# A sixth pair of gates by seven products, weights split ahead, and the attention bias by transfer, in a transformer layer

## The chip, the cores and the metric

The kernel runs on one core of a Trainium2 chip. The metric is the device time of one execution in microseconds (us), as the median of several runs. One further execution is recorded by the hardware profiler; all rows of the profile come from that one. Engines: PE is TensorE (matrix multiplication; PEld is its weight load), DVE is VectorE, ACT is ScalarE, POOL is GpSimd, and SP is the engine that issues all transfers here. "SPq" rows are its queue.

## The reference

One layer over 1024 tokens of width 1024. Two kinds of attention run side by side on the same input, and two sigmoid gates merge them:

```python
h = x @ w_in[l]
qa, ka, va, qb, kb, vb, ga, gb = jnp.split(h, split_pts, axis=-1)
y_a = chunk_band_attention(heads_a(qa), heads_a(ka), heads_a(va), rel_bias[l]) @ w_proj_a[l]
y_b = stick_breaking_attention(heads_b(qb), heads_b(kb), heads_b(vb)) @ w_proj_b[l]
gate_a = jax.nn.sigmoid(ga + b_gate[l, :D])
gate_b = jax.nn.sigmoid(gb + b_gate[l, D:])
mix = (gate_a * y_a + gate_b * y_b) @ w_out[l]
x = layer_norm(DEEPNORM_ALPHA * x + mix, ln1_g[l], ln1_b[l])
gu = x @ w_ffn_in[l]
g, u = jnp.split(gu, 2, axis=-1)
ffn = (jax.nn.silu(g) * u) @ w_ffn_out[l]
x = layer_norm(DEEPNORM_ALPHA * x + ffn, ln2_g[l], ln2_b[l])
```

Attention A (8 heads of 64) is a softmax over a band of 9 chunks of 64 tokens, with a learned bias `rel_bias[head, clip(distance)]` added to each score. Attention B (8 heads of 64) is strictly causal and has no softmax: a weight is a sigmoid times the running product of (1 - sigmoid) over the keys between. All values are float32.

## The kernel before

**Matmuls.** A float32 operand is split into a high and a low part (`split`, line 108: a ScalarE copy that rounds, and a VectorE subtraction for the rest). Each product is three matmuls: high x high, high x low, low x high. The whole program is laid out by a scheduler when it is built: it orders the instructions of each engine from the order in the code, the data they need and the buffers that come free. So the order in the code is a priority, and an instruction that is ready can move ahead of one that is not.

**Buffers.** On-chip memory is divided into tags (`SLOTS`, line 42) of equal buffers of 128 x 1024. Tags `qs`, `kh`, `kl` and `v` have two each; the helper `cycle` (line 71) deals them in turn during the projections, and attention uses the same tags for the heads' q, k (high), k (low) and v. PSUM has 8 banks (`BANKS`, line 43): 2 for fillers and products, 2 for scores, 3 for transposes, 1 for the value sum (`pv`).

**Projections.** The list `work` (line 228) has a pair of column panels per entry: q with k of two heads, v with v, and gate A with gate B. Each pair is computed by a seven-product scheme (`pair_steps`, line 183; products in the order 1, 2, 6, 5, 7, 3, 4) in place of eight: 7 x 12 = 84 matmuls of 512 columns in place of 96. Product 6 adds into the PSUM bank that ScalarE copied out after product 1. `run_pairs` (line 410) runs the list and loads the next weights in between. `N_GATE = 5` (line 236) gate pairs, ten of sixteen gates, are done here, and their sigmoid too (`out_g`, line 394). `small_inputs` (line 315) brings in the bias table, reversed, and the gate biases. Results go to memory and are loaded again per head.

**Attention.** `vsteps` (line 800) is a hand-written list of 12 steps a head: 8 in the first half of the queries (g = 0) and 4 in the second (g = 1). In each step the loop at line 821 does, in this order: due loads; due score blocks (`LEAD`, line 37, tells how many blocks must be out by which of the 12 steps); the step's transposes (`turn`, line 648) with their split on ScalarE and VectorE; some fillers; the value matmul (`mult`, line 657) of the step `LAG` = 2 back; some more fillers. The first `mult` of a half needs the one `pv` bank, which ScalarE empties after the last `mult` of the half before (line 679).

In A a score block (`soft_block`, line 573) is a sum with the bias and a running minimum on VectorE (line 582), an exponential on ScalarE (line 588), a reciprocal, and a division on GpSimd (line 593). The bias of a head (`rel_bias_tile`, line 556) is loaded with one row per partition, shifted by one, and then turned round and negated by ScalarE (line 562). In B a block (`stick_block`, line 607) is two sigmoids on ScalarE, a scan on VectorE and a product on GpSimd (line 628).

**Fillers.** `fill_all` (line 695) yields single matmuls of work that depends on no attention step: the gates that the projections left out (`gate`, line 453, 48 matmuls each) and then the projection of A's output (line 732, 24 for each of eight panels). `FILL = (18.0, 42.0)` is how many of them go to a head of A and of B. Their weights are loaded, copied by ScalarE (line 439) and subtracted by GpSimd (line 440) while attention runs. `later` (line 630) holds work that is due some steps on: the addition of the two halves of a head's output (line 683) and then, for the last pairs of heads, the split of that output (`split_y`, line 765: a ScalarE copy and a GpSimd subtraction).

After attention come the projection of B's output, the output projection, the first normalization, and the feed-forward part, which the change does not touch.

Of the kernel before, what the change touches and what calls it, by code (L numbers as in the profile page):

```python
# [11 lines left out]
F32 = mybir.dt.float32  # L12
F32R = mybir.dt.float32r
# [20 lines left out]


LAG = 2
LEAD = ((6, 7, 9, 9, 10, 10, 11, 11, 12, 12, 13, 13), (7, 8, 9, 9, 10, 10, 11, 11, 12, 12, 13, 14))

FILL = (18.0, 42.0)

# [5 lines left out]
def hybrid_trunk_kernel(ctx: ExitStack, tc, x, xt, w_in, b_gate, rel_bias, w_proj,  # L48
# [55 lines left out]
    ORDER = (1, 2, 6, 5, 7, 3, 4)  # L104
    s_dr = [[dram(f"s_dr{g}_{hf}_", 7) for hf in range(2)] for g in range(4)]
    rel_dr = dr.tile([8, 896], F32, name="rel_dr")

    def split(dst_h, dst_l, src):
        nc.scalar.copy(dst_h, src)  # L109
# [123 lines left out]
            if i % 2:  # L233
                work.append(("v", br * 4 + i - 1, br * 12 + 8 + i - 1, br * 12 + 8 + i))

    N_GATE = 5
    work += [("g", j, 24 + j, 32 + j) for j in range(N_GATE)]
    Wa = [dict() for _ in work]

# [3 lines left out]
    def right(i):  # L243
        prep_right(Wa[i], f"p{i}", w_in[work[i][3]], "op")
        prep_last(Wa[i], f"p{i}", "kp")
# [69 lines left out]
    def small_inputs():  # L315

        rel_sb = cycle(QKV, "rel_sb")[0:8, 0:896]
        rel_in = cycle(QKV, "rel_in")[0:8, 0:N_REL]
        dma(rel_in, rel_bias)
        nc.vector.tensor_copy(rel_sb[:, 383:896], rel_in[:, ::-1])  # L320
        nc.vector.tensor_copy(rel_sb[:, 0:383], rel_in[:, 512:513].to_broadcast([8, 383]))
        dma(rel_dr, rel_sb)
        dma(bg, b_gate)

    def store_hl(d, hi, lo):
# [30 lines left out]
    def project(i):  # L356
# [50 lines left out]

        return pair_steps(f"p{i}", Wa[i], ops_x, c, done, "pv" if i == 3 else "mm")

    def run_pairs(steps, left, right, also=lambda i: None, first=2, aside=lambda i: None,  # L410
                  then=lambda: None):

        n = len(steps)
        for j in range(first):
            steps[j][0]()
            steps[j][1]()
        then()
        for i in range(n):
            rest = steps[i][2:] if i < first else steps[i]
            for j, p in enumerate(rest):  # L420
                p()
                if j == 0 and i + 1 < n:
                    right(i + 1)
                if j == 1 and i + 2 < n:
                    left(i + 2)
                aside(i)
            also(i)
# [16 lines left out]
    def load_w(*args):  # L444
        return begin_w(*args)()

    def of(tag):
        return lambda name, dtype=F32: slot(tag, name, dtype)

    def begin_gate(i, lo_eng):  # L450
        return begin_w(w_in[24 + (i % 2) * 8 + i // 2], f"g{i}", of("op"), of("op"), lo_eng)

    def gate(i, w, half_way, freed=None):
# [49 lines left out]
    def rest_of_start():  # L503
# [3 lines left out]
        for kt in range(4):  # L507
# [2 lines left out]

    run_pairs([project(i) for i in range(1, len(work))],
              lambda i: left(i + 1) if i > 2 else left_again(3) if i == 2 else None,
              lambda i: right(i + 1), first=3, then=rest_of_start, also=lambda i: small_inputs() if i == 2 else None)
    first_gate = 2 * N_GATE
    first_w = begin_gate(first_gate, nc.vector)()


# [36 lines left out]
        return [t[0][:, 0:512], t[0][:, 512:896], t[1][:, 0:256], t[1][:, 256:384]]  # L554

    def rel_bias_tile(head):
        braw = slot("kp", f"braw{head}")
        src = rel_dr[head:head + 1, 0:640]
        dma(braw[:, 0:640],
            bass.AP(tensor=src.tensor, offset=src.offset, ap=[[1, P], [1, 640]]))  # L560
        bias = slot("kp", f"bias{head}")
        nc.scalar.activation(bias[:, 0:640], braw[:, 0:640][:, ::-1], AF.Copy, scale=-1.0)  # L562
        nc.gpsimd.memset(bias[0:DH, 576:640], BIG)  # L563
        nc.gpsimd.memset(bias[DH:P, 0:DH], BIG)
        return bias
# [66 lines left out]
    def value_steps(hd, g, wt):  # L632

        br, h = hd["br"], hd["h"]
        reach = (4, 8)[br]
        q0 = 4 * g
        nm = f"{'ab'[br]}{hd['n']}_{g}"
        pv = []

        kbs = [4, 5, 6, 7, 3, 2, 1, 0] if g == 0 else [7, 6, 5, 4]  # L640
        steps = []
        for i, kb in enumerate(kbs):
            lo_q = max(q0, kb - reach)
            hi_q = min(q0 + 3, kb)
            n = (hi_q - lo_q + 1) * P
            pts = []

            def turn(kb=kb, lo_q=lo_q, hi_q=hi_q, n=n, pts=pts):
                tp = bank("tr", f"tp_{nm}_{kb}")
                for qb in range(lo_q, hi_q + 1):  # L650
                    tr(tp[:, (qb - lo_q) * P:(qb - lo_q + 1) * P],  # L651
                       wt[qb - q0][:, (kb - qb) * P:(kb - qb + 1) * P], ident)
                pt = slot("pt", f"pt_{nm}_{kb}", F32R)
                split(pt[:, 0:n], pt[:, HW:HW + n], tp[:, 0:n])
                pts.append(pt)

            def mult(i=i, kb=kb, lo_q=lo_q, n=n, pts=pts):
                v = hd["v"]
                if i == 0:
                    pv.append(bank("pv", f"pv_{nm}"))  # L660
                last = i == len(kbs) - 1
                cs = slice((lo_q - q0) * P, (lo_q - q0) * P + n)
                pt = pts[0]
                mm(pv[0][:, cs], v[:, kb, :], pt[:, 0:n], start=(i == 0), stop=False)
                mm(pv[0][:, cs], v[:, kb, :], pt[:, HW:HW + n], start=False, stop=last)
                if last:
                    yt = hd["yt"]()
                    r = slice(h * DH, (h + 1) * DH)
                    gs = slice(g * HW, (g + 1) * HW)
                    if hd["i"] == 7:  # L670
                        nc.scalar.copy(yt[r, gs], pv[0][DH:P])
                        nc.vector.tensor_tensor(yt[r, gs], pv[0][0:DH], yt[r, gs], ALU.add)
                    else:

                        if g == 0:
                            hd["yv"] = slot("yt", f"yv_{nm}")
                        yv = hd["yv"]
                        both, other = (yt, yv) if h == 0 else (yv, yt)
                        nc.scalar.copy(both[:, gs], pv[0])
                        dma(other[r, gs], both[(DH, 0)[h]:(P, DH)[h], gs])  # L680

                        def add():
                            nc.gpsimd.tensor_tensor(yt[r, gs], yt[r, gs], yv[r, gs], ALU.add)
                            if h == 1 and g == 1:
                                if hd["i"] > 4:
                                    later.append([2, lambda: split_y(hd["i"], yt, nc.gpsimd)])
                                else:
                                    dma(y_dr[hd["i"]], yt)
                        later.append([3, add])

            steps.append((turn, mult))
        return steps


    def fill_all():
        w = first_w
        got = []
        for i in range(first_gate, 15):
            end = begin_gate(i + 1, nc.gpsimd)
            yield from gate(i, w, lambda: got.append(end()))  # L700
            w = got.pop()
        end = begin_proj(0, 0, "op", nc.gpsimd)
        ends = {}

        def freed(k):
# [9 lines left out]
        gates = {0: begin_gA(0)}  # L715
        for cc in range(4):
            if cc < 3:
                end = begin_proj(0, cc + 1, "op", nc.gpsimd)
            for j in range(2):
                c = 2 * cc + j  # L720
                t = gates.pop(c)
# [99 lines left out]
    for si, (hd, g, st, box) in enumerate(vsteps):  # L821
# [18 lines left out]
        goal += FILL[hd["br"]] / nhead  # L840
        fill_until(0.5 * (last + goal))
        pend.append(mult)
        if len(pend) > LAG:
            pend.pop(0)()
        fill_until(goal)
    for m_ in pend:
# [391 lines left out]
```

## Time and profile before

| What | us |
|---|---|
| median of 3 runs | 1454.58 (1454.35 to 1455.19) |
| the profiled execution | 1453.11 |
| its span, first to last instruction | 1451.1 |

The span falls into stages; TensorE's busy time in those that the change does not touch:

| Stage | from, to | TensorE busy |
|---|---|---|
| start | 0 to 30.0 | 28.07 of 30.0 |
| rest of B's output, output projection, first normalization | 662 to 812 | 149.00 of 150.0 |
| feed-forward, first part | 812 to 1207 | 395.00 of 395.0 |
| feed-forward, second part, and the end | 1207 to 1451.1 | 234.71 of 244.1 |

How to read rows: in a row by stretches, "393.89:409.90 16.01, 15.56 (x96) ..." is the stretch, its length, and then busy time (and number of instructions) of each engine named in the text. A row of waits has who waited, for whom, the total, how often, and the longest. A busy TensorE overlaps one matmul with the next, so spacing, not duration, is what a matmul costs.

### The profile page before, as it was taken

To read this page: it belongs to the slowest core of one execution; us is meant where nothing else is said; L and a number is where in the kernel's file an instruction comes from. 1 tells how busy PE (TensorE), PEld (TensorE's weight loads), DVE (VectorE), ACT (ScalarE), POOL (GpSimd) and SP (SyncE) were. 2 spreads that over 40 slices of the span, in tenths; PEclk is the share of its full clock that TensorE was granted. 3 is DMA by queue.
4 is the path that set the end of the run, shared out by engine and by line. 5 is a ranking of instruction groups with operands and counts; after the bars stand their busy time and mean duration, and the time that the engine had idled before them with its cause. 6 is when DMAs were issued, how large, how long until landed. Compare 5 with 4: busy or idle time off the path is not lost.

```text
span 1451.1 us, 19140 instructions
## 1 busy us (share of the span) xinstructions
PE 1429.5 (99%) x6748; PEld 1181.2 (81%) x6748; DVE 1024.4 (71%) x1644; ACT 682.7 (47%) x1187; POOL 278.9 (19%) x326
## 2 busy tenths in 40 slices
PE   9999999999999999999999999999999999999997
PEld 7888888888888788877888888888888887888886
DVE  8875565434776878877849966676677755978767
ACT  6444444446878878874313633444444433221201
POOL 0000000003655879850014000000000000100016
PEclk9999999999999999999999999999999999999999
DMA  7555545338667477647502123344444457787602
GB/s 247 156 178 174 174 148 186 110 101 255 196 191 199 131 226 229 204 178 239 186 25 94 66 102 114 134 159 160 160 159 145 151 197 250 286 307 242 205 15 102
DMA packets 83167, 246.15 MB, mean 170 GB/s; under 512 B 10480, under 2 KB 10480, under 8 KB 83072
## 3 DMA queue, kind: packets, MB, share of 16 engines
q1 hardware_dynamic: 83072, 244.94, 50.8%
q8 instruction: 53, 0.87, 0.2%
q14 instruction: 42, 0.34, 0.1%
HBM read 161.51 MB, written 79.72 MB: 166 GB/s over the span
## 4 chain that ended last, share of the span: by engine, by line
PE 90%; DVE 4%; ACT 2%; issue 1%; DMA 1%; POOL 1%; SPq 0%; POOLq 0%; DVEq 0%; ACTq 0%
PE sxf L179 15%; PE sxp L179 12%; PE szf L179 7%; PE dx L1171 6%; PE szp L179 6%; PE syf L179 4%; PE gps L460 4%; PE syp L179 3%; PE dz L1171 3%; PE yAps L732 2%; PE tp_b L651 2%; PE ops L119 2%; PE ops L117 2%; PE ops L116 2%; PE fpswh_h L116 2%; PE fpswh_h L119 2%
## 5 line engine op out<-in xcount | busy, mean ns | idle before, releaser
L1127 POOL TENSOR_TENSOR wdyt<-wdyt 128x512 f32<-128x512 f32 x8 | 10.7, 1336 | 515.7 <-DVE wdgt L1126 485.1
L628 POOL TENSOR_TENSOR w_b<-w_b,kp_b 128x511 f32<-128x511 f32 (+3 forms) x96 | 97.4, 1029 | 26.9 <-DVE kp_b L623 16.9
L623 DVE TENSOR_TENSOR_SCAN kp_b<-kp_b,ident_ps 128x512 f32<-128x512 f32 (+2 forms) x64 | 56.5, 883 | 24.9 <-ACT kp_b L620 24.6
L891 POOL TENSOR_TENSOR mv<-mv,neghalf 128x1 f32<-128x1 f32 x16 | 23.9, 1491 | 210.9 <-DVE mv L890 210.9
L563 POOL MEMSET bias<- 64x64 f32 x8 | 1.2, 145 | 327.8 <-ACT bias L562 327.8
L192 DVE TENSOR_TENSOR c<-sxp,c 128x512 f32<-128x512 f32 x16 | 11.1, 691 | 69.8 <-issue 40.2
L620 ACT ACTIVATE kp_b<-sc_b 128x512 f32<-128x512 f32 (+3 forms) x96 | 48.4, 504 | 23.9 <-PE sc_b L546 22.9
L110 DVE TENSOR_TENSOR pt_b<-tp_b,pt_b 128x512 fp32r<-128x512 f32 (+1 forms) x96 | 50.3, 543 | 8.4 <-ACT pt_b L109 7.7
L179 PE MATMUL szf<-x1S63h,wcf 128*128 128x512 f32 x168 | 55.1, 389 | 0.0
L1102 DVE TENSOR_TENSOR x<-dx,x 128x512 f32<-128x512 f32 x64 | 43.2, 686 | 15.5 <-PE dx L1171 15.5
L110 DVE TENSOR_TENSOR sl<-h,sl 128x512 fp32r<-128x512 f32 x56 | 38.4, 685 | 19.4 <-ACT sl L109 19.4
L593 POOL TENSOR_SCALAR w_a<-w_a,st_a 128x640 f32<-128x640 f32 (+2 forms) x64 | 42.8, 671 | 48.2 <-DVE st_a L592 33.0
L110 DVE TENSOR_TENSOR pt_a<-tp_a,pt_a 128x512 fp32r<-128x512 f32 (+1 forms) x96 | 45.8, 486 | 8.1 <-ACT pt_a L109 6.9
L651 PE MATMUL tp_b<-ident,w_b 128*128 128x128 f32 x288 | 47.7, 274 | 3.7 <-DVE pt_b L110 3.4
L109 ACT CAST pt_b<-tp_b 128x512 fp32r<-128x512 f32 (+1 forms) x96 | 47.3, 499 | 8.2 <-PE tp_b L651 7.4
L109 ACT CAST sl<-h 128x512 fp32r<-128x512 f32 x56 | 34.7, 620 | 33.7 <-PE syf L179 17.1
L116 PE MATMUL ops<-wh_o,mh 128*128 128x512 f32 x128 | 50.2, 392 | 0.0
L119 PE MATMUL ops<-wh_o,ml 128*128 128x512 f32 x128 | 50.0, 391 | 0.0
L117 PE MATMUL ops<-wl_o,mh 128*128 128x512 f32 x128 | 49.9, 390 | 0.0
L621 ACT ACTIVATE w_b<-sc_b 128x511 f32<-128x511 f32 (+3 forms) x96 | 48.5, 506 | 0.0
L109 ACT CAST pt_a<-tp_a 128x512 fp32r<-128x512 f32 (+1 forms) x96 | 40.0, 426 | 18.2 <-PE tp_a L651 16.9
L588 ACT ACTIVATE w_a<-w_a,st_a 128x640 f32<-128x640 f32 (+2 forms) x64 | 44.7, 698 | 5.2 <-DVE st_a L582 4.3
(1890 smaller groups left out, 4807.2 us busy)
## 6 DMA issues: line engine op xcount, KB each, us to landing
s_dr<-sl SPq DMA_DIRECT2D x112, 256.0 KB, 2.3
sd<-s_dr SPq DMA_DIRECT2D x56, 512.0 KB, 4.5
wLf<-in_w_ffn_in_dram SPq DMA_DIRECT2D x22, 512.0 KB, 4.5
wRf<-in_w_ffn_in_dram SPq DMA_DIRECT2D x22, 512.0 KB, 3.6
wRp<-in_w_in_dram SPq DMA_DIRECT2D x17, 512.0 KB, 4.7
wLp<-in_w_in_dram SPq DMA_DIRECT2D x17, 512.0 KB, 5.4
v_dr<-v SPq DMA_DIRECT2D x16, 512.0 KB, 4.5
kl<-k_dr SPq DMA_DIRECT2D x32, 256.0 KB, 5.4
```

What stands on the lines that cost most here:

```text
L109: nc.scalar.copy(dst_h, src)
L110: nc.vector.tensor_tensor(dst_l, src, dst_h.bitcast(F32), ALU.subtract)
L116: mm(acc, lh, rh, start=(i == 0), stop=False)
L117: mm(acc, lh, rl, start=False, stop=False)
L119: mm(acc, ll, rh, start=False, stop=(i == n))
L179: mm(acc, lw[:, ks], rx, start=(first and kt == i == 0), stop=(kt == 3 and i == 2), skip_group_check=not first)
L460: mm(acc[hf], lw[:, ks], rx[k][:, (LO, HI)[hf]], start=(k == j == 0), stop=(k == KT - 1 and j == 2))
L621: nc.scalar.activation(be[:, m0:e], sc[:, m0 - c0:n], AF.Sigmoid)
L623: nc.vector.tensor_tensor_scan(kp[:, 0:e], kp[:, 0:e], ident_ps()[:, 0:e], 0.0, ALU.mult, ALU.add)
L628: nc.gpsimd.tensor_tensor(be[:, m0:e], be[:, m0:e], kp[:, m0 - 1:e - 1], ALU.mult)
L651: tr(tp[:, (qb - lo_q) * P:(qb - lo_q + 1) * P], wt[qb - q0][:, (kb - qb) * P:(kb - qb + 1) * P], ident)
L1171: mm(acc, a, b, start=(first and i == n == 0), stop=(i == n - 1 == 1), skip_group_check=not first)
```

## The change

- `N_GATE` goes from 5 to 6: gates 10 and 11 move from the fillers to the seven-product list.
- `FILL` goes from (18, 42) to (8, 40): 8 x (8 + 40) = 384 fillers, 96 fewer.
- The weights of the fillers but the first gate's (gates 13, 14, 15 and four pairs of panels for A's output) are loaded, split and stored to memory in the last seven steps of the projections (`store_split`), and loaded in two parts when they are needed (`begin_split`).
- The bias table is negated by ScalarE when it is brought in, and not reversed. Eight transfers from memory to memory write it 128 times per head, each row one place further (a step of 1025 in rows of 1024). `rel_bias_tile` is then one plain load, without ScalarE's turn.
- `LEAD`: one score block of A a step earlier. In A the first value matmul of a head's second half is held back by one step, and two follow in the next. The split of an output of B waits 6 steps after its addition, not 2.

```diff
-LEAD = ((6, 7, 9, 9, 10, 10, 11, 11, 12, 12, 13, 13), (7, 8, 9, 9, 10, 10, 11, 11, 12, 12, 13, 14))
-FILL = (18.0, 42.0)
+LEAD = ((6, 8, 9, 9, 10, 10, 11, 11, 12, 12, 13, 13), (7, 8, 9, 9, 10, 10, 11, 11, 12, 12, 13, 14))
+FILL = (8.0, 40.0)
...
+    skew_dr = [dr.tile([P + 1, 1024], F32, name=f"skew_dr{h}") for h in range(8)]
...
-    N_GATE = 5
+    N_GATE = 6
...
-        nc.vector.tensor_copy(rel_sb[:, 383:896], rel_in[:, ::-1])
-        nc.vector.tensor_copy(rel_sb[:, 0:383], rel_in[:, 512:513].to_broadcast([8, 383]))
+        nc.scalar.activation(rel_sb[:, 0:513], rel_in, AF.Copy, scale=-1.0)
+        nc.scalar.activation(rel_sb[:, 513:896], rel_in[:, 512:513].to_broadcast([8, 383]),
+                             AF.Copy, scale=-1.0)
         dma(rel_dr, rel_sb)
+        for h in range(8):
+            src, dst = rel_dr[h:h + 1, 128:896], skew_dr[h][0:1, 128:896]
+            dma(bass.AP(tensor=dst.tensor, offset=dst.offset, ap=[[1025, P], [1, 768]]),
+                bass.AP(tensor=src.tensor, offset=src.offset, ap=[[0, P], [1, 768]]))
...
+    first_gate = 2 * N_GATE
+
+    def aside_work(i):
+        if i == 2:
+            small_inputs()
+        first = len(work) - 1 - len(ws_dr)
+        if i >= first:
+            store_split(i - first)
...
+    ws_dr = [dram(f"ws_dr{i}_", 2) for i in range(15 - 2 * N_GATE + 4)]
+
+    def store_split(i):
+        n = 15 - 2 * N_GATE
+        if i < n:
+            j = 2 * N_GATE + 1 + i
+            srcs = w_in[24 + (j % 2) * 8 + j // 2]
+        else:
+            srcs = [(cs, w_proj[2 * (i - n) + j][:, 0:HW]) for j, cs in enumerate((LO, HI))]
+        take = lambda name, dtype=F32: cycle(QKV, name, dtype)
+        for d, t in zip(ws_dr[i], load_w(srcs, f"pre{i}", take, take, nc.vector)):
+            dma(d, t.bitcast(F32))
+
+    def begin_split(i, name):
+        hl = [slot("op", f"w{p}_{name}", F32R) for p in "hl"]
+        for d, t in zip(ws_dr[i], hl):
+            dma(t.bitcast(F32), d)
+        return lambda: hl
...
     def begin_gate(i, lo_eng):
+        if i > first_gate:
+            return begin_split(i - first_gate - 1, f"g{i}")
...
-              lambda i: right(i + 1), first=3, then=rest_of_start, also=lambda i: small_inputs() if i == 2 else None)
-    first_gate = 2 * N_GATE
+              lambda i: right(i + 1), first=3, then=rest_of_start, also=aside_work)
...
-        braw = slot("kp", f"braw{head}")
-        src = rel_dr[head:head + 1, 0:640]
-        dma(braw[:, 0:640],
-            bass.AP(tensor=src.tensor, offset=src.offset, ap=[[1, P], [1, 640]]))
         bias = slot("kp", f"bias{head}")
-        nc.scalar.activation(bias[:, 0:640], braw[:, 0:640][:, ::-1], AF.Copy, scale=-1.0)
+        dma(bias[:, 0:640], skew_dr[head][0:P, 256:896])
...
-                                    later.append([2, lambda: split_y(hd["i"], yt, nc.gpsimd)])
+                                    later.append([6, lambda: split_y(hd["i"], yt, nc.gpsimd)])
...
-        end = begin_proj(0, 0, "op", nc.gpsimd)
+        end = begin_split(15 - first_gate, "y0_0")
...
-                end = begin_proj(0, cc + 1, "op", nc.gpsimd)
+                end = begin_split(16 - first_gate + cc, f"y0_{cc + 1}")
...
-        if len(pend) > LAG:
+        wait = hd["br"] == 0 and (g, st) == (1, LAG)
+        while len(pend) > LAG + wait:
             pend.pop(0)()
```

## The prediction

> **What bounds the kernel now.** I read the page's first part, then the chain of work that ended last, then the busy time by stage.
>
> ```profile
> span 1451.1 us, 19140 instructions
> PE 1429.5 (99%) x6748; PEld 1181.2 (81%) x6748; DVE 1024.4 (71%) x1644; ACT 682.7 (47%) x1187; POOL 278.9 (19%) x326
> PE 90%; DVE 4%; ACT 2%; issue 1%; DMA 1%; POOL 1%; SPq 0%; POOLq 0%; DVEq 0%; ACTq 0%
> ...
> 30.00:342.90 312.90, 312.77 (x1409) 257.89 (x1408) 180.63 (x243) 141.52 (x198) 2.99 (x5) 1.00 0.52 160
> 342.90:483.00 140.10, 135.35 (x816) 114.79 (x815) 107.12 (x366) 116.23 (x286) 82.10 (x115) 1.00 0.67 195
> 483.00:662.00 179.00, 174.58 (x969) 146.43 (x969) 141.32 (x204) 139.58 (x307) 132.15 (x165) 1.00 0.61 191
> ```
>
> TensorE carries 90% of the chain. The three stretches are the projections, attention A and attention B; their columns are length, then busy time of TensorE, weight load, VectorE, ScalarE and GpSimd, then clock, DMA share and GB/s. Outside the projections the other engines are close behind: in A VectorE and ScalarE are busy for 107 and 116 of 140 us. So a matmul taken out is worth its spacing only while TensorE stays the last engine, and I read the stages one by one.
>
> Two rows of the chain in order of time give the spacing in the projections:
>
> ```profile
> 332.30 2.72 PE szp L179 x12
> 335.02 2.72 PE sxp L179 x12
> ```
>
> Twelve matmuls of 512 columns take 2.72 us, or 0.2267 us each. For A I cut the stage into heads, from one first value matmul of a second half to the next; the second group of rows counts only the gate fillers of line 460. The last row is one B head.
>
> ```profile
> 363.39:377.51 14.12, 13.47 (x87) 11.81 (x87) 11.77 (x47) 12.23 (x34) 9.16 (x14) 1.00 0.69 190
> 393.89:409.90 16.01, 15.56 (x96) 13.57 (x96) 12.27 (x46) 13.00 (x33) 7.98 (x13) 1.00 0.84 250
> 409.90:425.91 16.01, 15.55 (x96) 13.56 (x96) 12.27 (x46) 12.58 (x33) 8.24 (x13) 1.00 0.62 183
> ...
> 342.90:363.39 20.49, 8.20 (x25) 4.32 (x25) 1.00 0.81 238
> ...
> 363.39:377.51 14.12, 3.99 (x9) 1.70 (x9) 1.00 0.69 190
> 393.89:409.90 16.01, 7.60 (x18) 3.40 (x18) 1.00 0.84 250
> ...
> 528.00:550.00 22.00, 22.00 (x125) 18.62 (x124) 16.83 (x24) 20.05 (x44) 19.64 (x24) 1.00 0.79 249
> ```
>
> These rows already hold the main experiment. A head with 18 fillers takes 16.01 us; one that happened to get 9 took 14.12. Nine fillers are worth 1.89 us, against 9 x 0.2267 = 2.04 by spacing. VectorE is busy for 12.27 us of a head: that is the floor if TensorE gets out of its way.
>
> **The change part by part.**
>
> *Gate pair six.* Two gates leave the attention fillers: 2 x 48 = 96 matmuls, 80 of them from A (8 heads x 10) and 16 from B (8 x 2). They come back as seven products of 12, 84 matmuls, in the projections, where TensorE has no gaps: +84 x 0.2267 = +19.04 us. Out of A go 80 x 0.2267 = 18.14, out of B 16 x 0.2267 = 3.63. Net -2.72 us if every filler was on the path. With 8 fillers an A head would take 14.12 - 0.23 = 13.89 us, still 1.6 above VectorE's floor.
>
> *Shifted steps in A.* The change issues one score block a step earlier and holds the first value matmul of a head's second half back by one step. The waits of A:
>
> ```profile
> PEld sc_a L545 <- DVE st_a L582: 4.7, 11, 0.7
> PEld pv_a L664 <- ACT yt L679: 2.5, 5, 0.8
> PE sc_a L545 <- DVE st_a L582: 2.0, 6, 0.5
> PEld pv_a L664 <- ACT yv_a L679: 1.4, 3, 0.5
> PE pv_a L664 <- ACT yt L679: 0.7, 2, 0.5
> ```
>
> The value matmul waits for ScalarE to empty the only value bank (4.6 us in these rows); the scores wait for VectorE to free one of two banks (6.7 us). Weight loads run ahead, so not all of this is lost time. The held step covers the first kind; the earlier block breaks up a step that asked for three score banks. Bounds: 0 and -11.3. I take -4.5, nearest the 4.6 of the value bank and little of the rest, because the score bank is still freed by VectorE.
>
> *Less cover in A.* What the fillers hid now shows: a step of a head falls from 16.01/12 = 1.33 us to about 1.1, and a value matmul comes two steps after its transpose, so ScalarE's and VectorE's splits have 2.2 us where they had 2.7. The 14.12 us head shows only 0.15 us of this (2.04 less 1.89). With the waits above cured a head would take 13.89 - 4.5/8 = 13.33 us. Bounds: 0, and 8 x (14.12 - 13.33) = +6.3 if no head gets under the shortest one seen. I take +2, nearer to 0 as that head lost so little.
>
> *Weights split ahead, bias by transfer.* These take work out of attention:
>
> ```profile
> L562 ACT ACTIVATE bias<-braw x8: 722/740/767, 320.9 to 415.9; 128x640 f32<-128x640 f32 x8
> L439 ACT CAST wh_g<-wr_g x6: 1047/1048/1063, 328.2 to 447.1; 128x1024 fp32r<-128x1024 f32 x6
> L440 POOL TENSOR_TENSOR wl_g<-wr_g,wh_g x5: 2374/2404/2406, 337.8 to 470.2; 128x1024 fp32r<-128x1024 f32 x5
> L440 DVE TENSOR_TENSOR wl_g<-wr_g,wh_g x1: 1224/1224/1224, 329.4 to 329.4; 128x1024 fp32r<-128x1024 f32 x1
> ```
>
> ScalarE loses eight flips of 0.74 us; nine weight splits (1.05 us there, 2.40 on GpSimd) go, two because the gates are gone and seven into the projections. There they cost 7 x 1.05 on ScalarE and 7 x 1.22 on VectorE, in seven steps of 19.04 us where TensorE is covered: ScalarE is busy for 141.5 and VectorE for 180.6 of 312.9 us. Were one of them to stand in front of the copy of the first product, TensorE would wait, since the third product adds into the same bank: the slack is one product, 2.72 us, less a copy. Bounds 0 and 7 x 2.7 = 19; I take +0.5, since the seven loads need nothing but a free buffer. The transfers: each weight is read once (0.5 MB), written and read as 1 MB, so 10.5 MB in 133 us or 79 GB/s on top of 160 at a DMA share of 0.52, about 0.78 together. The eight skewed bias copies add 8 x 393 KB both ways, early, behind one more wait on SP for the small bias write; the loads of the next weights stand behind it. Nothing of before shows a transfer from memory to memory; between 0 and one late weight load I take 0.
>
> *Later y split in B.* The views of the waits, first around 571 to 595, then 610 to 634:
>
> ```profile
> PEld tp_b L651 <- POOL yl L769: 1.3, 1, 1.3
> PE tp_b L651 <- DVE pt_b L110: 1.0, 1, 1.0
> ...
> ACT yh L768 <- POOL yt L683: 3.0, 1, 3.0
> PE tp_b L651 <- DVE pt_b L110: 2.1, 3, 1.0
> ```
>
> ScalarE stood 3.0 us before the split of y, waiting for GpSimd's addition; the splits of the weights behind it came late, and TensorE after them. Four steps later (22.00/12 = 1.83 us each, 7.3 us) the addition is long done. What is late next is GpSimd's own 2.4 us of subtraction. The TensorE waits in the fence are 4.4 us; bounds 0 and -4.4, and I take -2.5.
>
> *The start of A.* The buffers for q, k and v are also those of the projections' results, dealt in turn over the tags qs, kh, kl and v. Counting the helper's turns through the changed code from 0, the first result of the last gate pair is number 88 and the low half of the last split weight is 92; both are multiples of four, so both fall on the tag "qs", which has two buffers. So both heads' q loads stand behind them. Before, only the second head's did:
>
> ```profile
> 345.83 0.32 SPq L397 DMA_DIRECT2D g_dr<-c  x1
> 346.25 1.42 SPq L530 DMA_DIRECT2D kh<-k_dr  x2
> 350.40 0.86 SPq L527 DMA_DIRECT2D qs<-q_dr  x2
> ...
> qs<-q_dr SPq DMA_DIRECT2D x16, 512.0 KB, 4.9
> ```
>
> The last products ended at 342.9, the store left at 345.83, and the q load at 350.40, landing 4.9 us later: 12.4 us after the products. If that happens to the first head, its scores start 12.4 us late. The 48 matmuls of the first filler gate (10.9 us) can be pulled in front, as seven were already (25 instead of 18 in the row of 342.90), but they are then missing as cover. Bounds 0 and +12.4. I take +3, since the split of a weight depends on no product and can free its buffer early.
>
> **Sum.** -2.72 - 4.5 + 2 + 0.5 - 2.5 + 3 = -4.2 us. The profiled execution took 1453.11, 1.5 below the median of 1454.58 and 2.0 above its span; so it becomes 1448.9, and the median 1450.4.
>
> **The rivals.**
>
> *Late queries (slower).* The first scores wait the full 12.4 us and the fillers spent there leave the heads short later. The row of 350.40 speaks for it, the freedom of the order against it. Price: 12.4 in place of 3, so -4.2 + 9.4 = +5.2, 1459.8. It turns the sign from 7.2 us of wait on. [...]
>
> *Short cover.* Heads stay near 14.1 us because VectorE (12.27 us busy, in order) cannot be fed more closely. Then the cured waits come back as others: +6.3 in place of 2 gives +0.1, 1454.7. For it: VectorE would be busy for 12.27 of 13.3 us; against it: the 9-filler head lost almost nothing.
>
> *All waits cured.* Late start and cover 0, A's waits -7 (midway between the value bank's 4.6 and most of the 11.3), B's -3: -2.72 - 7 - 3 = -12.7, 1441.9. For it: the fences of waits; against it: they count waits that overlap.
>
> *Blocked ScalarE in the projections.* One 2.7 us stall a split would be +19, 1469; the ordinary prefetch of weights there speaks against it.
>
> [...]
>
> **How the numbers follow.** Forecast 0.45 (1446 to 1453 its own range), late queries 0.24, short cover 0.16, all cured 0.10, blocked ScalarE 0.04, clock 0.01. A measurement of this kernel tells 0.2%, or 2.9 us, from no change, so faster means under 1451.7 and slower above 1457.5. Of the forecast 0.39 lies below 1451.7 and 0.06 between; short cover splits into 0.02, 0.12 and 0.02; late queries give 0.04 between and 0.20 above, as fillers may cover a part. With all cured that makes 0.51 faster; 0.06 + 0.12 + 0.04 = 0.22 the same; 0.02 + 0.20 + 0.05 = 0.27 slower. The range, 1443 to 1461, reaches over the late queries and down to the cured waits, and leaves out the last two and part of the cured ones.
>
> **What would show it.** Right: seven products more, ending near 362; A heads of 13 to 14 us with 8 fillers; no value wait of 0.3 us in A; no ScalarE wait of 3.0 us for the addition in B. Wrong: TensorE idle, or 40 and more fillers, between the last product and the first scores; heads of 14 us or more; ScalarE or TensorE waiting in the projections for the weight loads, or for the skewed copies.

## The result, and the profile after

The changed kernel takes 1460.16 us (median of 6 runs, 1458.52 to 1464.26) against 1454.88 us for the kernel before on the same chip: a ratio of 1.0042, interval 1.0032 to 1.0052. It is slower by 5 to 6 us. Faster was forecast, 1450.4; the time lies inside the range of 1443 to 1461, but only because the range reached up for late queries, which did not come. The profiled execution took 1461.1 us, 1.8 us more than its span. First the parts and the chain of the page after:

```profile
span 1459.3 us, 19182 instructions
PE 1431.4 (98%) x6736; PEld 1182.1 (81%) x6736; DVE 1037.2 (71%) x1660; ACT 677.5 (46%) x1181; POOL 257.1 (18%) x317
PE 89%; DVE 4%; DMA 2%; ACT 2%; issue 1%; POOL 1%; SPq 0%; POOLq 0%; DVEq 0%; ACTq 0%
```

TensorE has twelve matmuls less and still 1.9 us more of busy time. The loss is found by stages: A from the last product to the first value matmul of B, then B to its last one. Length and TensorE's busy time are the first two figures; before, then after.

```profile
343.02:485.10 142.08, 136.98 (x824) 115.91 (x822) 108.56 (x368) 118.23 (x289) 84.04 (x117) 1.00 0.67 196
485.10:661.25 176.15, 172.07 (x956) 144.60 (x957) 139.12 (x200) 136.95 (x303) 130.20 (x163) 1.00 0.61 191
```

```profile
363.40:490.57 127.17, 119.82 (x739) 100.33 (x738) 105.19 (x368) 105.27 (x274) 73.21 (x110) 1.00 0.74 220
490.57:668.36 177.79, 171.39 (x947) 143.59 (x946) 139.03 (x200) 132.17 (x297) 121.42 (x160) 0.99 0.65 200
```

- Up to the last product: 343.02 to 363.40, +20.4. The 84 products are 19.04 of it; the rest, 1.3 us, goes with a stretch of 3.4 us at half clock in the first 13 us, shown in the last section. The kernel before had none there: its clock was 1.00 from 0 to 13 us.
- A: -14.9. It lost 84 fillers (158 to 74), 19.04 by spacing (0.2267 us each, where the record of one lasts 0.39); 4.1 did not come back. 2.9 of that lie in the first three heads: 46.04 us with 37 fillers before (353.80 to 399.84), 42.60 with 9 after (373.63 to 416.23), where 28 fillers are 6.35.
- B: +1.6, with 12 fillers less (-2.7): 4.3 us did not come back. TensorE's idle time rose by 2.3 of them (4.08 to 6.40), and a stretch of 3.4 us at half clock (589.5 to 593.0, clock 0.51) took up to 1.7, half its length.
- The rest, by difference from the span: +1.1. In all +8.2. The medians differ by 5.3 only: some 3 us of this table belong to these two executions, the half clock at the start among them.

Four of A's heads after, three of 8 fillers behind one of 2, and two of B:

```profile
401.42:416.23 14.81, 12.53 (x81) 10.49 (x81) 10.90 (x44) 11.50 (x32) 8.35 (x15) 1.00 0.70 209
430.13:444.83 14.70, 14.05 (x88) 11.99 (x88) 12.04 (x48) 11.53 (x32) 7.47 (x12) 1.00 0.79 239
444.83:458.79 13.96, 13.53 (x87) 11.67 (x87) 11.72 (x45) 11.73 (x32) 8.48 (x12) 1.00 0.73 222
458.79:472.73 13.94, 13.48 (x86) 11.47 (x85) 11.66 (x44) 11.25 (x31) 6.98 (x14) 1.00 0.77 238
...
557.97:579.86 21.89, 21.89 (x126) 18.82 (x125) 18.94 (x28) 16.43 (x40) 17.76 (x25) 1.00 0.91 268
579.86:605.93 26.07, 24.16 (x126) 19.71 (x124) 18.85 (x28) 17.80 (x41) 17.16 (x23) 0.93 0.64 200
```

The clean heads of A are at 13.94, the 13.89 that was worked out for 8 fillers without any wait cured. The head with 2 fillers is the longest. B's clean head takes 21.89 us, all of it busy, much like the 22.00 before; the next one is 4 us longer. The waits of A after; the last three rows are of its first three heads alone, one of the changed kernel and then two of e3 below, which has no earlier score block:

```profile
PEld sc_a L580 <- DVE st_a L613: 4.8, 13, 0.7
PEld tp_a L682 <- DVE pt_a L111: 2.5, 5, 1.0
PEld tp_a L682 <- POOL w_a L624: 2.5, 5, 0.8
PEld pv_a L695 <- ACT yt L710: 1.9, 3, 0.8
PEld pv_a L695 <- ACT yv_a L710: 1.7, 4, 0.6
PE sc_a L581 <- DMA kl<-k_dr: 1.2, 1, 1.2
...
PE sc_a L580 <- DVE st_a L613: 1.2, 3, 0.5
...
PE sc_a L580 <- DVE st_a L613: 0.5, 1, 0.5
PE sc_a L581 <- DMA kl<-k_dr: 1.0, 1, 1.0
```

The value bank's wait (L710) is still there, and the scores' too. Transposes now wait for VectorE's split and for GpSimd's division (L624), and one score block waits for the low half of its keys. That last wait lies in the head of 14.81 us. Its chain in the timeline, on ScalarE, SP's queue, GpSimd, SP again and TensorE (start, duration, and in brackets the idle time before and its releaser):

```profile
400.69 0.58 ACT L710 COPY yv_a<-pv_a 128x512 f32<-128x512 f32 x1
...
401.29 0.48 SPq L711 DMA_DIRECT2D yt<-yv_a  x1
...
407.24 1.29 POOL L714 TENSOR_TENSOR yt<-yt,yv_a 64x512 f32<-64x512 f32 x1 [2.85 <-PE tp_a L682]
408.62 2.35 POOL L624 TENSOR_SCALAR w_a<-w_a,st_a 128x640 f32<-128x640 f32 x3
...
408.55 0.33 SPq L719 DMA_DIRECT2D y_dr<-yt  x1
408.94 1.24 SPq L565 DMA_DIRECT2D kl<-k_dr  x2
...
415.62 0.53 PE L581 MATMUL sc_a<-kl,qs 128*128 128x320 f32 x2 [1.20 <-DMA kl<-k_dr]
```

Half an output is moved, GpSimd adds it 6 us after the move was issued (its wait of 2.85 us is put down to a transpose here, and to the transfer in e13), the store follows the addition, and the keys' low half stands behind the store on SP's queue. Three divisions stand behind the same addition on GpSimd. In B, ScalarE's split of y still waits for GpSimd's addition. The first two rows are the head of 26.07 us, the third is the whole of B. The last is the split in the same head of the kernel before, where it waited 0.49 us; the 3.0 of the prediction stood in a later head:

```profile
ACT yh L799 <- POOL yt L714: 2.8, 1, 2.8
PE tp_b L682 <- DVE pt_b L111: 1.5, 1, 1.5
...
ACT yh L799 <- POOL yt L714: 6.3, 2, 3.4
...
580.79 1.05 ACT L768 CAST yh<-yt 128x1024 fp32r<-128x1024 f32 x1 [0.49 <-POOL yt L683]
```

### The profile page after: what moved, and what is told of

Read it like the earlier page. It is cut to its first block, busy times and chain, and to the rows that moved or that the text cites. A ratio compares the mean times of both kernels' runs of the same rounds, so it can differ in the third digit from the quotient of the medians.

```text
span 1459.3 us, 19182 instructions
## 1 busy us (share of the span) xinstructions
PE 1431.4 (98%) x6736; PEld 1182.1 (81%) x6736; DVE 1037.2 (71%) x1660; ACT 677.5 (46%) x1181; POOL 257.1 (18%) x317
## 4 chain that ended last, share of the span: by engine, by line
PE 89%; DVE 4%; DMA 2%; ACT 2%; issue 1%; POOL 1%; SPq 0%; POOLq 0%; DVEq 0%; ACTq 0%
PE sxf L180 15%; PE sxp L180 12%; PE szf L180 7%; PE dx L1203 6%; PE szp L180 6%; PE syf L180 4%; PE syp L180 3%; PE dz L1203 3%; PE gps L496 2%; PE yAps L763 2%; PE tp_b L682 2%; PE ops L120 2%; PE ops L118 2%; PE ops L117 2%; PE fpswh_h L117 2%; PE fpswh_h L120 1%
## 5 line engine op out<-in xcount | busy, mean ns | idle before, releaser
L624 POOL TENSOR_SCALAR w_a<-w_a,st_a 128x640 f32<-128x640 f32 (+2 forms) x64 | 42.4, 667 | 61.9 <-DVE st_a L623 28.5
L682 PEld LDWEIGHTS tp_b<-ident,w_b 128*128 128x128 f32 x288 | 35.4, 141 | 14.5 <-issue 3.5
```

What stands on the lines that cost most here:

```text
L682: tr(tp[:, (qb - lo_q) * P:(qb - lo_q + 1) * P], wt[qb - q0][:, (kb - qb) * P:(kb - qb + 1) * P], ident)
```

## The experiments

Each was timed beside the kernel before in five rounds. "Mended" below means e5's two edits. For comparison: the changed kernel is at 1.0042. The kernel before had medians of 1454.1 to 1454.5 us beside these runs and 1454.9 beside the changed kernel, so a difference of medians between two runs is uncertain by about as much.

**e1, five pairs again.** Isolates the steps from the sixth pair.

```diff
-FILL = (8.0, 40.0)
+FILL = (18.0, 42.0)
-    N_GATE = 6
+    N_GATE = 5
```

> The changed kernel with five gate pairs by products and 18 and 42 fillers again; the shifted steps, the weights split ahead and the bias by transfer stay. Theory 'cover' (the loss comes from moving the sixth pair: fewer fillers in A and B cover less): this kernel is within 2 us of the kernel before, 1453 to 1456.5. Rival 'other parts' (the transfers and the work moved into the projections cost the time): 4 us or more above before, 1459 and up.

1456.61 us, ratio 1.0015 (1.0007 to 1.0024): just above the range expected. The steps, the weights ahead and the bias together gain nothing and cost some 2 us. Heads of A take 16.01 us with 18 fillers, as before, and the fifth B head 25.32 (23.55 before). So that head gets longer without the sixth pair, too.

```profile
416.16:432.17 16.01, 15.60 (x97) 13.46 (x97) 11.99 (x46) 11.34 (x31) 7.84 (x10) 1.00 0.62 186
...
575.25:600.57 25.32, 23.19 (x128) 19.05 (x127) 19.66 (x29) 17.80 (x42) 17.80 (x25) 1.00 0.65 193
```

**e2, the sixth pair alone**, in the kernel before (`N_GATE = 6`, `FILL = (8.0, 40.0)`).

> The kernel before with the sixth gate pair by products and 8 and 40 fillers, and nothing else of the change. Theory 'cover': 4 to 8 us above before, 1459 to 1463, with A heads of about 14 us and TensorE waits of 20 us or more in A. Rival 'other parts': 2 to 3 us below before, about 1452, as 12 matmuls of 0.227 us are fewer.

1464.2 us, ratio 1.0070 (1.0057 to 1.0083), above even the slower of the two expectations. One B head takes 29.28 us, and its waits show why: ScalarE stands 6.7 us before the copy of a weight, for GpSimd's split of y, and the transposes' copies stand behind it.

```profile
532.78:562.06 29.28, 22.51 (x125) 18.60 (x123) 17.20 (x24) 21.09 (x45) 28.64 (x29) 0.94 0.64 196
...
DVE pt_b L110 <- ACT pt_b L109: 8.4, 3, 8.0
ACT wh_y L439 <- POOL yl L769: 6.7, 1, 6.7
```

GpSimd is busy for 28.64 of the 29.28 us: this is what splitting the weights ahead removes (e7).

**e7, weights split in attention** as before, the rest of the change kept (the branches to `store_split` and `begin_split` taken out).

> The changed kernel, but the weights of the fillers are loaded whole and split in attention, as before. With the gate move alone at 9.7 us and the whole change at about 5.5 us over before, the other parts saved about 4: if that is the splitting ahead (1.05 us of ScalarE and 2.40 of GpSimd for each of seven weights out of attention), this is 3 to 5 us slower than the changed kernel, 1463 to 1465. If it is the bias by transfer, within 1.5 us of the changed kernel.

1464.05 us, 1.0066 (1.0054 to 1.0079): splitting ahead saves 3.9 us of the changed kernel. Its loss lies in B (187.66 us; 186.45 in e2). By e2, 1464.2, the steps and the bias together are worth nothing beside late weights.

**e3, no earlier score block.**

```diff
-LEAD = ((6, 8, 9, 9, 10, 10, 11, 11, 12, 12, 13, 13), (7, 8, 9, 9, 10, 10, 11, 11, 12, 12, 13, 14))
+LEAD = ((6, 7, 9, 9, 10, 10, 11, 11, 12, 12, 13, 13), (7, 8, 9, 9, 10, 10, 11, 11, 12, 12, 13, 14))
```

> The changed kernel without the earlier score block. If the earlier block puts ScalarE's exponential in front of the copy of the value bank (the 0.5 us wait of each A head), its absence brings that wait back to 0.3 us and the score wait to 0.47: about the same total, within 2 us of the changed kernel. If the earlier block cured something, 3 us or more slower than the changed kernel.

1456.9 us, 1.0016 (1.0008 to 1.0025): the earlier block costs 3.3 us, which neither expectation had. By the profiles A is 1.7 us shorter without it (125.51 to 127.17), and its first three heads 2.15 (40.45 to 42.60, both with 9 fillers). The rows above say where: the score bank's wait falls from 1.2 to 0.5 us. The keys' wait stays, at 1.0 for 1.2, so it is not the block's.

**e11, the other two steps undone** (`wait = 0`; the y split 2 steps after the addition).

> The changed kernel with two of its shifted steps undone: the value matmul not held, the split of y after 2 steps. If the scheduler that lays out the program puts these instructions in the same places with and without the two edits, as the waits of 0.5 and 3 us in front of them suggest, the time is the changed kernel's within 1 us, 1459 to 1461. If the two edits did something, 2 us or more away.

1459.78 us, 1.0034 (1.0024 to 1.0044): the same as the changed kernel. The built programs show it too: with 2 or with 6 steps, the order of instructions on all five engines is identical, and undoing the held value matmul swaps one pair of neighbouring instructions. Beside the other parts the scheduler puts them in the same places either way. This holds for the changed kernel only: either edit alone, made in the kernel before, does change the built order, and neither was timed there.

**e12, bias turned by ScalarE** as before (no skewed copies).

> The changed kernel with the bias turned round and negated by ScalarE in each A head (0.74 us) as before, and no copies from memory to memory. If that work off ScalarE is what the rest of the saved 4 us was, 2 to 4 us slower, 1462 to 1464; if the earlier splitting accounts for all, within 1 us of the changed kernel; if the memory copies or their wait cost time in the projections, faster.

1459.49 us, 1.0030 (1.0019 to 1.0042), 0.7 under the changed kernel, within the intervals: the transfer neither gains nor costs.

**e4, two outputs of B more through memory**, those of pairs 5 and 6 like that of pair 4: their split reads what was loaded back, and does not stand behind GpSimd's addition.

```diff
-                                if hd["i"] > 4:
+                                if hd["i"] > 6:
...
-                if c == 0:
-                    end_y = begin_y(4, nc.gpsimd)
-                elif c == 1:
+                if c in (0, 2, 5):
+                    end_y = begin_y({0: 4, 2: 5, 5: 6}[c], nc.gpsimd)
+                elif c in (1, 3, 6):
```

> The changed kernel, but the outputs of the sixth and seventh pair of heads go through memory and are split when the panels of A's projection are at numbers 2 and 5, as the earlier pairs' are. The copy that ScalarE waits 2.8 and 3.4 us for is then far from GpSimd's addition. If that wait costs TensorE what stands behind it (1.6 + 0.6 us and 1.5 + 1.3 us, and the half clock after the first): 4 to 6 us below the changed kernel, 1454 to 1456. If the waits only go elsewhere, as ScalarE and GpSimd have the same work: within 1.5 us of the changed kernel.

1455.78 us, 1.0009 (1.0001 to 1.0018): 4.4 us less. The long head is clean, and a later one, now of 26.61 us (25.31 in the changed kernel), has a new wait, ScalarE for a gate that is loaded late:

```profile
580.67:602.67 22.00, 22.00 (x125) 18.71 (x124) 18.67 (x28) 16.99 (x40) 16.23 (x22) 1.00 0.84 271
...
635.90 1.15 ACT L805 ACTIVATE gA<-gA,bg 128x1024 f32<-128x1024 f32 x1 [2.37 <-DMA gA<-g_dr]
```

**e8, fillers back to A** (`FILL = (14.0, 34.0)`).

> The changed kernel with 14 fillers a head in A and 34 in B, the same sum of 384. If A's waits are what too few fillers leave uncovered, A loses less: heads of 14.8 to 15.2 us rather than 13.9 + 1.36 = 15.3; B's heads fall from 22.0 by 1.36 to 20.6 where TensorE sets their length. Total 1 to 4 us below the changed kernel. If B has no room either (ScalarE 18 and GpSimd 17 to 19 us busy of 22), B falls by less than 6 x 0.227 a head and the total is the same or worse, 1460 to 1464.

1455.33 us, 1.0012 (1.0003 to 1.0021): 4.9 us less with the same work, more than expected. The stages tell what a filler costs in each:

```profile
363.27:497.03 133.76, 128.36 (x785) 108.74 (x784) 107.39 (x369) 107.71 (x277) 74.17 (x111) 1.00 0.76 223
497.03:662.85 165.82, 159.80 (x899) 133.36 (x898) 138.96 (x199) 129.77 (x295) 120.65 (x159) 1.00 0.64 203
```

46 fillers moved. A grew by 6.6 us, 0.14 each, and B shrank by 12.0, 0.26 each, where the spacing is 0.2267. In A part of them fills time in which TensorE waited anyway: its idle time falls from 7.35 to 5.40 us. In B more than the spacing comes back; the stretch at half clock is gone there (clock 1.00 in the row above, 0.99 in the changed kernel), and the rest stays open.

**e5, two mendings**: e3's edit, and one output of B more through memory (pair 5, as in e4). **e6**: the same with five pairs and 18 and 42 fillers.

> The changed kernel without the earlier score block, and with the output of the sixth pair of heads (alone) through memory. If the two costs found so far are separate places (about 3.3 us in A, about 4 us in the fifth head of B), they add: 7 us below the changed kernel, 1451.5 to 1454, at or below the kernel before. If both were the same thing (one slow stretch, met or missed), no better than the better of the two alone, 1455.5 to 1457.

> The same two mendings with five gate pairs and 18 and 42 fillers. If the sixth pair, with the known waits cured, is worth its 12 matmuls (2.7 us), this is 1 to 3 us slower than the kernel with six and the same mendings. If the shorter cover in A eats that and more (A's TensorE waits rose from 18 to 22 us), it is 1 to 3 us faster, 1450 to 1453.

e5: 1453.69 us, 0.9999 (0.9990 to 1.0008). e6: 1451.53 us, 0.9985 (0.9976 to 0.9993), the fastest kernel of all and faster than before by some 2.2 us. The stages of e5, then of e6:

```profile
362.28:486.63 124.35, 118.52 (x739) 100.46 (x737) 105.50 (x368) 104.53 (x274) 74.06 (x111) 1.00 0.76 228
486.63:660.53 173.90, 169.65 (x945) 142.59 (x946) 138.59 (x200) 131.78 (x297) 120.43 (x159) 1.00 0.67 208
```

```profile
342.65:481.94 139.29, 135.17 (x823) 115.75 (x821) 108.03 (x368) 111.85 (x279) 73.56 (x110) 1.00 0.73 224
481.94:658.37 176.43, 172.89 (x960) 144.66 (x959) 139.19 (x200) 134.41 (x300) 120.72 (x160) 1.00 0.65 206
```

This is the sixth pair by itself, with the waits out of the way: A gives back 14.94 us for 84 fillers (0.178 each), B 2.53 for 12, and the projections cost 19.04. The sum is +1.6 us where counting matmuls gives -2.7; the medians differ by 2.2. A head of e6 with 18 fillers takes 15.59 us:

```profile
399.39:414.98 15.59, 15.28 (x98) 13.56 (x97) 12.24 (x46) 12.14 (x32) 9.26 (x15) 1.00 0.79 241
```

**e9 and e10, six pairs mended, other fillers** (e5 with `FILL` (14, 34) and (12, 36)).

> Six gate pairs, without the earlier score block, the sixth pair's output through memory, and 14 and 34 fillers. If the three costs found are separate (3.3 in A's order, about 3 in the fifth head of B, 4.9 by too few fillers in A), they add to some 10 us below the changed kernel: 1449 to 1451, faster than five pairs with the same mendings (1451.5). If the fillers in A cover the same waits that the earlier block made, 1452 to 1454.

> The same with 12 and 36. A filler moved from B to A gained 4.9 / 48 = 0.1 us each; between 8 and 14 fillers a straight line puts this a third of the way back, 1.5 us above the kernel with 14 and 34. If the gain comes only once the steps' own chain is covered, it is at least as fast as that one or 4 us slower.

1454.43 us, 0.9996 (0.9987 to 1.0005), and 1453.65 us, 0.9992 (0.9983 to 1.0001). Neither differs from e5 clear of the intervals, so the 4.9 us of e8 and the mendings are largely the same waits: the gains do not add up. The best six-pair kernels are level with the kernel before and stay 2.1 us above e6 by the medians, though the intervals of e10 and e6 still overlap.

**e13, e14, e15, the stores by GpSimd.** The store in the chain above (L719) is issued by GpSimd behind its addition, so that no keys stand behind it: in the changed kernel, in e5 and in e6.

```diff
-                                    dma(y_dr[hd["i"]], yt)
+                                    nc.gpsimd.dma_start(out=y_dr[hd["i"]], in_=yt)
```

> The changed kernel, with the stores of A's finished outputs issued by GpSimd, right behind its addition, and no longer by SP ahead of the next keys. Theory: the keys' low half comes in time, the wait of 1.2 us for it goes and the first three heads fall from 42.6 to 40.5 us or less; the time falls by 2 to 3 us, to about 1457.5. Rival (the loss is in the order of ScalarE's work, which the earlier block changes): the first three heads stay above 42 us, and the time within 1 us of 1460.2.

> The kernel of e5 (no earlier block, one more output of B through memory) with the same stores by GpSimd. Theory (the earlier block costs what it does by making that store late): little is left to gain, within 1 us of 1453.7, and e13 and this one stand closer together than the changed kernel and e5 do. Rival: the store costs something of its own, 1451 to 1452.

> The kernel of e6 (five pairs, 18 and 42 fillers, both mendings) with the same stores by GpSimd. With 18 fillers a head the keys come in time anyway: within 1 us of 1451.5. If the store holds up other transfers too, 1450 or less; if the issue by GpSimd delays its own work, 1452.5 or more.

Each is 6 to 9 us slower than its kernel without the edit: 1467.02 us (1.0086, 1.0073 to 1.0100), 1462.42 (1.0059, 1.0045 to 1.0073) and 1457.51 (1.0028, 1.0017 to 1.0038). Theory and rival both miss the time. In e13 the wait for the keys is gone, but GpSimd's addition waits 4.0 us for the moved half, and TensorE for the division behind it. The waits in e13's first heads of A:

```profile
PE tp_a L682 <- POOL w_a L624: 2.7, 2, 2.3
POOL yt L714 <- DMA yt<-yv_a: 4.0, 1, 4.0
```

The edit took in the stores of B's outputs too, and there ScalarE waits for outputs that are loaded back; the waits of B in e15, 527.59 to 603.13:

```profile
ACT yh L799 <- DMA yraw<-y_dr: 7.3, 2, 4.2
```

In e14 and e15 A is as long as without the edit (124.44 and 139.34 us), so all of their loss lies in B. These runs therefore test the chain badly. What e13 shows is that the store is not the only late link: the move ahead of it can be late as well.

**e16, e17, e18, the addition later.** The addition in A 8 steps after the copy and not 3, which puts every store behind the next keys on SP's queue: in the changed kernel, in e5 and in e6.

```diff
-                        later.append([3, add])
+                        later.append([8 if hd["br"] == 0 else 3, add])
```

> The changed kernel with the addition of A's halves 8 steps after the copy and not 3; every store of an output of A then stands behind the next keys on SP's queue. Theory (transfer, addition, store and keys are one chain that comes late in short heads): no wait for the keys' low half, the first three heads fall from 42.6 us to 40.5 or less, the time to about 1457.5. Rival (ScalarE's order, which the earlier block changes): the first three heads stay above 42 us, the time within 1 us of 1460.2.

> The kernel of e5 with the same later addition. Theory: within 1 us of 1453.7, since its keys were in time (the first three heads took 39.5 us). If the additions also held up divisions in the later heads, these fall under 13.6 us on the mean and the time to 1452.5 or less.

> The kernel of e6 (five pairs, 18 and 42 fillers) with the same later addition. The heads of 15.6 us hide the chain, so within 1 us of 1451.5; 1450.5 or less if the additions held up divisions there too.

1457.92 us (1.0028, 1.0018 to 1.0038), 1454.3 (0.9996, 0.9987 to 1.0005) and 1452.48 (0.9991, 0.9982 to 1.0000). In e16 the wait for the keys is gone and the time is about 2 us less; the interval still overlaps that of the changed kernel. By the profiles A is only 0.8 us shorter (126.38). The first three heads take 41.96 us, between the two expectations (42.60 after, 40.45 in e3): what the earlier block costs them is mostly still there, in waits for the score bank and for GpSimd's divisions. Without the earlier block (e17) and with 18 fillers (e18) the edit gains nothing.

## Why the prediction was wrong, point by point

Two steps failed by their mechanism: the shifted steps in A (-4.5) and the later y split in B (-2.5) were booked as 7.0 us of gain. Both took rows of waits as time on the path and a moved line of code as a moved instruction. In the changed kernel two of the three moves do nothing (e11), and the third costs 3.3 us (e3). One term had the right sign and was too small, the cover that A loses.

**Gate pair six: the count right, its worth wrong.** 84 products cost 19.04 and TensorE had no gaps there. But a filler taken out of A was worth 0.178 us (e5 against e6), not 0.2267. *Less cover in A* was the term for that, +2 in bounds of 0 to +6.3; the same two kernels give 19.04 - 14.94 = 4.1. I took it from one head with 9 fillers that lost 0.15 us. For a short head that was a fair sample, since 13.94 us came where 13.89 was worked out. The long heads beside it were not: with the weights split ahead and without the earlier block a head of 18 fillers takes 15.6 us (e6) and not 16.01, so ten fillers are worth less. From the fourth head on, e5 gives back 7.94 us for 53 fillers of e6, 12.0 by spacing, and that is all of the loss.

**Shifted steps in A: failed.** -4.5 was forecast. The held value matmul changed nothing in the changed kernel (e11), and the value bank's wait is still there. The earlier block did what it says and costs 3.3 us by the medians (e3). The profiles place 2.15 us of that in the first three heads, with a longer wait for the score bank. The rest is not placed, and why an earlier block makes that wait longer is open. It is no fixed price: with the weights split late A takes 124.85 us with the block (e7) and 125.62 without (e2). The chain of transfer, addition, store and keys is a cost of its own: its wait is there without the block (e3), is gone in e5 and e16, and does not occur in the kernel before. The bounds of 0 and -11.3 left out a loss, for which no reason stood there.

**Later y split in B: failed.** -2.5 was forecast and the bounds were 0 and -4.4. In the changed kernel a larger number of steps changes nothing (e11), and ScalarE still waits: 2.8 us in the fifth head, where it was 0.49, and 3.4 in a later one, where it was 3.0. Taking the wait away in another manner gained 4.4 us (e4), but that only gave back what the change had lost: B then takes 173.4 us, which is the 176.15 of the kernel before less the spacing of 12 fillers. So the rows of waits of the kernel before held no gain of 2.5. What lengthens the wait in the fifth head stays open; it comes with five pairs as well (e1).

**Weights split ahead, bias by transfer: right in the projections, not counted in attention.** The seven splits are covered in the projections, where TensorE's busy time is 0.25 us less than the length as it was 0.13 before:

```profile
30.00:363.40 333.40, 333.15 (x1498) 274.80 (x1497) 197.62 (x261) 154.22 (x213) 0.87 (x6) 1.00 0.62 199
```

What they buy in attention, 3.9 us (e7 against the changed kernel), was not counted: e2's stall of 6.7 us comes with the shorter heads. The bias is worth nothing that the intervals show (e12).

**The start of A, and the late queries.** The first score follows the last product at once, at 363.40, so the +3 and the 12.4 us of the rival did not come. That rival gave 1459.8, next to the measured time, and it is refuted all the same. That the time lies in the range is luck for the same reason.

**Short cover** came nearest in kind: heads of 13.9 to 14.8 us. It lay at 1454.7 because the cure in B stood in its sum. *Blocked ScalarE* and *all waits cured* did not occur, and no head of A in the changed kernel's profile shows a slower clock: it was 1.00 from 363.40 to 490.57. The 0.01 booked for *clock*, a lower clock in A for its fewer fillers, has no run behind it: A's mean is 1.00 in e3, e5, e6 and e8 as well, with 8 to 18 fillers a head, and the one lower figure at hand there, 0.76 in e4 from 414 to 421, lies in a single stretch of 7 us.

**The sum, from the profiles.** Forecast -4.2, profiled +8.2, a difference of 12.4 us by stages: up to the last product 20.4 against 19.5 (+0.8); A -14.9 against -18.14 - 4.5 + 2 + 3 = -17.6 (+2.7); B +1.6 against -3.63 - 2.5 = -6.1 (+7.8); the rest +1.1 against 0. B is the largest, and its 7.8 are the cure that did nothing (2.5), 0.9 for four fillers that left A and not B, and 4.4 of longer waits and slower clock. Of these the one stretch at half clock is at most 1.7, and the lower clock lies elsewhere in the profiles of e4 (0.76 from 414 to 421) and e2 (0.94 from 532.78 to 562.06).

The kept profiles take A apart more cleanly. It is 142.08 us before, 139.29 in e6 (the rest of the change without the earlier block), 124.35 in e5 (84 fillers fewer) and 127.17 in the changed kernel. So the rest of the change gained 2.8 us that were not forecast, the fillers brought 14.9 and not 19.0, and the earlier block with the keys' wait lost 2.8.

## What to carry to other kernels

Where a scheduler orders the program, compare the built order of instructions before costing a step that only moves code: undoing two of the three moved steps here left the order all but the same. Price an instruction that fills a waiting engine by whole stages at two counts of fillers, not by its spacing, which was 0.2267 us where A gave back 0.178. And before a wait is charged to an edit, look for it without the edit: the keys' wait stands in the head that the earlier block lengthened, and it was 1.0 us without that block, too.

## What was not expected of the hardware

The granted clock fell to half in short stretches. In the long B head TensorE waited 0.41 and 1.48 us. The timeline of the kernel after there, and then three stretches of it, the first from the start of the program (the third figure from the end is the granted clock):

```profile
587.68 0.47 PE L580 MATMUL sc_b<-kh,qs 128*128 128x448 f32 x1 [0.41 <-ACT w_b L652]
...
589.83 0.66 PE L682 MATMUL tp_b<-ident,w_b 128*128 128x128 f32 x2 [1.48 <-DVE pt_b L111]
590.72 0.63 PE L695 MATMUL pv_b<-pt_b,v 128*128 128x512 f32 x1
591.14 0.63 PE L696 MATMUL pv_b<-pt_b,v 128*128 128x512 f32 x1
```

```profile
9.30:12.70 3.40, 3.40 (x8) 2.72 (x9) 3.32 (x5) 3.14 (x6) 0.00 (x0) 0.50 1.03 405
587.00:590.00 3.00, 1.11 (x5) 0.50 (x5) 3.00 (x5) 3.00 (x8) 3.00 (x6) 0.92 0.55 201
589.50:593.00 3.50, 3.17 (x9) 2.58 (x10) 2.83 (x5) 1.03 (x4) 2.18 (x6) 0.51 0.99 258
```

From 587 to 590 TensorE is busy for 1.11 of 3 us, and then matmuls of 512 columns are 0.42 us apart in place of 0.2267. Here 1.48 us in one piece, with a wait of 0.41 us ahead, came before a drop that lasted some 3.4. At the start of the program no wait was even that long: the longest in the 3.4 us ahead of the drop was 0.79 us, with TensorE busy for 2.16 of them.

So one long wait is not what these two drops have in common. They are the only ones in the trace of the changed kernel ahead of its last matmul; the trace of the kernel before has none there (clock 1.00 from 0 to 1443.0). Each lasted 3.4 us (9.3 to 12.7 and 589.6 to 593.0), and in a stretch of that length ahead of them TensorE was busy for 2.16 and 1.78 us. The reverse does not hold: from 636.0 to 639.4 TensorE was busy for 1.61 us, and the clock stayed at 1.00 then and from 639.4 to 642.8. In e4 and e2 the mean clock was 0.76 over the 7 us from 414 to 421 and 0.94 over the head of 29.28 us; as an estimate from these, that is 3.4 us at half clock (2 x 0.24 x 7) and 3.5 us (2 x 0.06 x 29.28).

Such a drop is a cost beside the wait ahead of it: from 9.29 to 12.71 TensorE has 8 matmuls in 3.42 us, from 12.71 to 16.10 it has 16 in 3.39, so the 3.4 us at half clock did 1.7 us of work. The profiled executions differ in it: mean clock 0.999 and a span of 1448.7 us in e6, 0.996 and 1459.3 in the changed kernel, 0.994 and 1463.1 in e2. That idle stretches and the lower clock occur together is seen; that the one causes the other was not tried by itself.
